# Up projections of both MLPs as seven block products in place of eight

## The chip, the cores and the metric

The kernel runs on one NeuronCore of a Trainium2 chip. The metric is the device time of one execution in microseconds (us). Before the change three executions took 3145.03, 3157.53 and 3156.45 us, a median of 3156.45.

## The reference

One step of a two-layer decoder trunk on 1032 tokens (a prompt of 1024 and eight single new tokens), with D = 1024 and a hidden width of 4096. Layer 0 mixes tokens with a gated DeltaNet and a retention group, layer 1 with a Mamba-2 mixer; behind each mixer stand an output projection and the MLP that the change touches. All is float32.

```python
def squared_relu_mlp(h, w1, w2):
    a = jax.nn.relu(jnp.einsum('bld,df->blf', h, w1))
    return jnp.einsum('blf,fd->bld', a * a, w2)

for layer in range(DEPTH):          # DEPTH = 2
    ...
    x = x + out                     # out: the mixer's projection
    x = x + squared_relu_mlp(rms_norm(x, norm_mlp[layer]), mlp_w1[layer], mlp_w2[layer])
```

## The kernel before, in words

Activations lie transposed: 8 tiles of 128 features by 1032 tokens. Each float32 operand of a large product is held as two parts of the type fp32r, a rounded one (`hi`) and what is left (`lo`). `mm3` (L147) makes one product of 128 features out of three matmuls, hi·hi, hi·lo and lo·hi, with the weights as the stationary operand. `xh` and `xl` hold the parts of the normed activations for the whole kernel (16 tiles).

`load_w` (L135) brings 128x512 weights on SP's DMA queue into one of three `raw` buffers; ScalarE (ACT) rounds them into `whi`, and VectorE (DVE) or GpSimd (POOL) subtracts to get `wlo`. There are buffers for three such pairs (tag `hl`). Products land in PSUM: three banks `pg`, three `pm`, two `ps2`.

`out_proj` (L1335) adds the last blocks of the output projection to eight sum tiles `acc`, which stay in SBUF for the MLP, and splits each finished piece into `xh` and `xl`.

`mlp` (L1216) holds two loops in one. `up(t)` makes one of 32 tiles of 128 hidden features: 8 blocks of features by 3 token slices of 344 columns by 3 matmuls, 72 matmuls. Its eviction clips at zero and multiplies with the norm's factor `rstd_bc` on DVE, squares on ACT (`ahi`) and again on POOL, and subtracts on DVE (`alo`). The parts of hidden tiles stay in SBUF, 14 buffers of 1032 columns. Behind `up(4)`, `up(8)` and so on stands `down(b)`, which adds the products of four hidden tiles to `acc`: 8 output tiles by 3 slices by 4 blocks by 3 matmuls, 288 in all. So no hidden tile leaves the chip. Layer 1 ends with `finish`, which folds the final norm into the last block.

The code is written in one order, and a scheduler sets each engine's order from it; buffers come free when their last reader is done. Each engine then works strictly in its order.

Of the kernel before, what the change touches and what calls it, by code (L numbers as in the profile page):

```python
# [10 lines left out]
F32 = mybir.dt.float32  # L11
F32R = mybir.dt.float32r
# [6 lines left out]
P = 128  # L19
# [47 lines left out]
BLOCK_STEPS = [32, 64]  # L67
HF = 15
SHF = 8
RATE = (0.5, 0.6, 1.5, 0.5, 0.6)  # L70
DG = 2
DS = 2
# [23 lines left out]
class Kern:  # L96
# [330 lines left out]
    def layer(self, l):  # L427
        tc = self.tc
        nk = 16 if l else 8
        with ExitStack() as es:  # L430
            if l == 0:
                self.resid = lambda m: self.I["xT"][:, m, :]
            else:
                self.resid = lambda m: self.resd[m]
            dp = es.enter_context(tc.tile_pool(name=f"spill{l}", bufs=1, space=bass.MemoryType.DRAM))
            self.spill = [dp.tile([P, SEQ], F32, name=f"spill{l}_{k}") for k in range(nk)]
            self.egd = dp.tile([32, SEQ], F32, name=f"egd{l}")
            self.accd = [dp.tile([P, T], F32, name=f"accd{l}_{m}") for m in range(KT)]
            op = es.enter_context(tc.tile_pool(name=f"dec{l}", bufs=1))
            self.dmix = op.tile([P, nk, NDEC], F32, name=f"dmix{l}")  # L440
            name, blocks = ("wos" if l else "woh"), OUT_BLOCKS[l]
            with ExitStack() as es_op:
                with tc.tile_pool(name=f"mixb{l}", bufs=1, side="right", reuse_waits="tile") as gb:
                    with tc.tile_pool(name=f"mixa{l}", bufs=1, reuse_waits="tile") as ga:
                        mixers = (self.ssm_mixers if l else self.hyb_mixers)(Pools(ga, gb))
                        next(mixers)
                    tp = es_op.enter_context(tc.tile_pool(name=f"op{l}", bufs=1, reuse_waits="tile"))
                    next(mixers)
                    parts = self.load_block(blocks[1], tp)
                    for _ in mixers:  # L450
                        pass
                ap = es.enter_context(tc.tile_pool(name=f"acc{l}", bufs=1, side="right", reuse_waits="tile"))
                acc = [ap.tile([P, T], F32, name=f"acc{l}_{m}") for m in range(KT)]
                self.out_proj(name, blocks, acc, tp, parts, "mlp%d" % l)
            self.mlp(l, acc, l == 1)

    def load_block(self, block, tp, pool=None):
        parts = []
# [754 lines left out]
        yield  # L1213


    def mlp(self, l, acc, last):  # L1216
        nc, tc, I = self.nc, self.tc, self.I
        with tc.tile_pool(name=f"mlp{l}", bufs=1, reuse_waits="tile") as tp:
            ssq = self.rstd_bc
            parts = {}  # L1220

            def up(t):
                hi = tp.tile([P, T], F32R, tag="a2", name="ahi", bufs=14)
                lo = tp.tile([P, T], F32R, tag="a2", name="alo", bufs=14)
                parts[t] = (hi, lo)

                def ev(n, ps):
                    s = NSL[n]
                    r = tp.tile([P, NW], F32, tag="r", name="r", bufs=4)
                    nc.vector.scalar_tensor_tensor(out=r, in0=ps, scalar=0.0, in1=self.rstd_bc[:, s], op0=ALU.max, op1=ALU.mult)  # L1230
                    nc.scalar.activation(hi[:, s], r, AF.Square)  # L1231
                    nc.gpsimd.tensor_tensor(out=r, in0=r, in1=r, op=ALU.mult)  # L1232
                    nc.vector.tensor_tensor(out=lo[:, s], in0=r, in1=hi[:, s].bitcast(F32), op=ALU.subtract)  # L1233
                self.gemm_tile(I["w1"][l, t], 128, ev, t == 1)

            def down(b):
                ks = range(4 * b, 4 * b + 4)

                def ev(m, n, ps):
                    s = acc[m][:, NSL[n]]  # L1240
                    nc.vector.tensor_tensor(out=s, in0=s, in1=ps, op=ALU.add)  # L1241
                    if b == HID // 4 - 1:
                        self.split_piece(m, n, s, ssq, tp, "mix1")
                        if n == 2:
                            nc.gpsimd.dma_start(self.resd[m], acc[m])
                for _ in self.gemm_flush(lambda m: I["w2"][l, b, m], [parts.pop(k) for k in ks], ev):
                    pass
            def finish(b):

# [2 lines left out]
                for m in range(KT):  # L1252
                    dst = None
                    if m < 5:
                        w = tp.tile([P, T], F32R, tag="a2", name="wfin", bufs=14)
                        dst = (w[:, 0:512], w[:, 512:1024])
                    ws.append(self.load_w(I["w2"][l, b, m], 512, nc.gpsimd, dst))
                def norm(s0, s1, sqs):
# [62 lines left out]
                    pend = norm(s0, s1, sqs)  # L1321
                for _ in pend:
                    pass
            for t in range(HID):
                up(t)
                if t % 4 == 0 and t:
                    down(t // 4 - 1)
            if last:
                finish(HID // 4 - 1)
            else:  # L1330
# [4 lines left out]
    def out_proj(self, name, blocks, acc, tp, parts, norm):  # L1335
# [3 lines left out]
        with tc.tile_pool(name="oq" + name, bufs=1, side="right", reuse_waits="tile") as tq:  # L1339
# [3 lines left out]
            for i in range(1, len(blocks)):  # L1343
# [3 lines left out]
                def ev(m, n, ps):  # L1347
                    o = acc[m][:, NSL[n]]
                    nc.vector.tensor_tensor(out=o, in0=o, in1=ps, op=ALU.add)  # L1349
                    if last:  # L1350
                        self.split_piece(m, n, o, ssq, tp, norm)
                for _ in self.gemm_flush(lambda m: self.I[name][m, :, c0 * 128:c0 * 128 + w], cur, ev):
                    pass
            self.rstd = self.rstd_from()
# [587 lines left out]
```

## Time and profile before

| what | value |
| --- | --- |
| device time, median of three | 3156.45 us |
| the profiled execution: its own time | 3153.58 us |
| the profiled execution: its span | 3151.8 us |
| matmuls in the span | 19702 |
| ACT busy | 830.7 us (26%) |
| HBM traffic | 174.78 MB read, 43.24 MB written |
| large weight loads of both MLPs (`raw<-w`) | 256, of 256 KB each, median 2.6 us to landing |

How to read it: the page counts an engine as busy while an instruction is in it. Matmuls overlap in the array, so the time that one takes (325 ns for 344 columns) is not the time until the next starts; for that the start times in the timeline have to be subtracted. PEld is the load of the stationary operand, which runs beside the matmuls. "PEclk" is the share of TensorE's clock that was granted.

### The profile page before, as it was taken

To read this page: it belongs to the slowest core of one execution; us is meant where nothing else is said; L and a number is where in the kernel's file an instruction comes from. 1 tells how busy PE (TensorE), PEld (TensorE's weight loads), DVE (VectorE), ACT (ScalarE), POOL (GpSimd) and SP (SyncE) were. 2 spreads that over 40 slices of the span, in tenths; PEclk is the share of its full clock that TensorE was granted. 3 is DMA by queue.
4 is the path that set the end of the run, shared out by engine and by line. 5 is a ranking of instruction groups with operands and counts; after the bars stand their busy time and mean duration, and the time that the engine had idled before them with its cause. 6 is when DMAs were issued, how large, how long until landed. Compare 5 with 4: busy or idle time off the path is not lost. (4 is left out here: it accounts for less than half of the span.)

```text
span 3151.8 us, 48807 instructions
## 1 busy us (share of the span) xinstructions
PE 3031.0 (96%) x19702; PEld 2908.6 (92%) x19702; DVE 1662.4 (53%) x3127; ACT 830.7 (26%) x1577; POOL 922.8 (29%) x940
## 2 busy tenths in 40 slices
PE   8999999989999999999998999999899999999998
PEld 6888888878999999999997989898899999999997
DVE  7664657554333333334778686868435333333334
ACT  4222222214211111113343434343114111111112
POOL 2121214114222112224135444445224222221124
PEclk9899989989999999999999999999999999999999
DMA  4011103153111111112222222224721111111112
GB/s 129 21 49 55 48 22 105 62 178 107 45 47 48 48 48 47 48 48 74 79 66 77 78 98 78 96 77 141 247 74 46 46 48 47 48 48 48 48 47 71
DMA packets 119186, 223.32 MB, mean 71 GB/s; under 512 B 14064, under 2 KB 43504, under 8 KB 118960
## 3 DMA queue, kind: packets, MB, share of 16 engines
q1 hardware_dynamic: 110512, 190.80, 20.0%
q0 software_dynamic: 8448, 29.40, 2.4%
q8 instruction: 155, 2.54, 0.3%
q14 instruction: 71, 0.58, 0.1%
HBM read 174.78 MB, written 43.24 MB: 69 GB/s over the span
## 5 line engine op out<-in xcount | busy, mean ns | idle before, releaser
L148 PE MATMUL pg<-xh,whi 128*128 128x344 f32 x3072 | 999.0, 325 | 2.3 <-DVE z L1525 2.3
L150 PE MATMUL pg<-xh,wlo 128*128 128x344 f32 x3072 | 995.1, 324 | 0.0
L149 PE MATMUL pg<-xl,whi 128*128 128x344 f32 x3072 | 994.6, 324 | 0.0
L142 ACT CAST whi<-raw 128x512 fp32r<-128x512 f32 (+2 forms) x443 | 270.8, 611 | 1215.2 <-PE pg L149 1137.8
L148 PEld LDWEIGHTS pg<-xh,whi 128*128 128x128 f32 x3072 | 582.6, 190 | 9.1 <-DVE z L1525 3.1
L150 PEld LDWEIGHTS pg<-xh,wlo 128*128 128x128 f32 x3072 | 582.7, 190 | 3.4 <-issue 2.3
L149 PEld LDWEIGHTS pg<-xl,whi 128*128 128x128 f32 x3072 | 581.6, 189 | 3.1 <-issue 2.0
L149 PE MATMUL pg<-alo,whi 128*128 128x344 f32 (+2 forms) x1476 | 472.8, 320 | 0.0
L150 PE MATMUL pg<-ahi,wlo 128*128 128x344 f32 (+2 forms) x1476 | 472.7, 320 | 0.0
L148 PE MATMUL pg<-ahi,whi 128*128 128x344 f32 (+2 forms) x1476 | 472.0, 320 | 0.0
L1241 DVE TENSOR_TENSOR acc<-acc,pg 128x344 f32<-128x344 f32 x360 | 183.1, 512 | 387.9 <-PE pg L150 387.7
L143 POOL TENSOR_TENSOR wlo<-raw,whi 128x512 fp32r<-128x512 f32 (+2 forms) x179 | 224.8, 1257 | 507.7 <-ACT whi L142 505.9
L1232 POOL TENSOR_TENSOR r<-r 128x344 f32<-128x344 f32 x192 | 145.9, 760 | 755.3 <-ACT ahi L1231 707.6
L143 DVE TENSOR_TENSOR wlo<-raw,whi 128x512 fp32r<-128x512 f32 x264 | 192.8, 730 | 194.0 <-ACT whi L142 188.1
L150 PEld LDWEIGHTS pg<-ahi,wlo 128*128 128x128 f32 x1476 | 277.9, 188 | 0.0
L148 PEld LDWEIGHTS pg<-ahi,whi 128*128 128x128 f32 x1476 | 277.8, 188 | 0.0
L149 PEld LDWEIGHTS pg<-alo,whi 128*128 128x128 f32 x1476 | 277.6, 188 | 0.0
L1233 DVE TENSOR_TENSOR alo<-r,ahi 128x344 fp32r<-128x344 f32 x192 | 134.7, 702 | 253.6 <-POOL r L1232 253.6
L1231 ACT ACTIVATE ahi<-r 128x344 fp32r<-128x344 f32 x192 | 94.5, 492 | 340.9 <-DVE r L1230 340.9
L148 PE MATMUL pg<-mhi,whi 128*128 128x344 f32 x408 | 132.1, 324 | 8.9 <-DVE acc L1349 6.0
L1230 DVE SCALAR_TENSOR_TENSOR r<-pg,rstd_bc 128x344 f32<-128x344 f32 x186 | 94.9, 510 | 79.4 <-PE pg L150 78.0
L150 PE MATMUL pg<-mhi,wlo 128*128 128x344 f32 x408 | 131.7, 323 | 0.0
(547 smaller groups left out, 4184.7 us busy)
## 6 DMA issues: line engine op xcount, KB each, us to landing
raw<-w SPq DMA_DIRECT2D x256, 256.0 KB, 2.6
raw<-wis SPq DMA_DIRECT2D x80, 256.0 KB, 2.8
raw<-wih SPq DMA_DIRECT2D x56, 256.0 KB, 2.8
mraw<-spill SPq DMA_DIRECT2D x17, 512.0 KB, 4.6
accd<-ost SPq DMA_DIRECT2D x48, 172.0 KB, 3.1
acc<-accd SPq DMA_DIRECT2D x16, 516.0 KB, 7.0
EG<-egd SPq DMA_DIRECT2D x32, 256.0 KB, 6.3
dS<-sstate SPq DMA_DIRECT2D x32, 256.0 KB, 7.1
```

The source lines that it names most:

```text
L142: nc.scalar.copy(hi[:, :n], raw[:, :n])
L143: (lo_eng or nc.vector).tensor_tensor(out=lo[:, :n], in0=raw[:, :n], in1=hi[:, :n].bitcast(F32), op=ALU.subtract)
L148: t.matmul(ps, lhsT=whi, rhs=xhi, start=start, stop=False)
L149: t.matmul(ps, lhsT=whi, rhs=xlo, start=False, stop=False)
L150: t.matmul(ps, lhsT=wlo, rhs=xhi, start=False, stop=stop)
L1230: nc.vector.scalar_tensor_tensor(out=r, in0=ps, scalar=0.0, in1=self.rstd_bc[:, s], op0=ALU.max, op1=ALU.mult)
L1231: nc.scalar.activation(hi[:, s], r, AF.Square)
L1232: nc.gpsimd.tensor_tensor(out=r, in0=r, in1=r, op=ALU.mult)
L1233: nc.vector.tensor_tensor(out=lo[:, s], in0=r, in1=hi[:, s].bitcast(F32), op=ALU.subtract)
L1241: nc.vector.tensor_tensor(out=s, in0=s, in1=ps, op=ALU.add)
```

## The change

Hidden tiles t and t+16 are now made together, as a pair. The weights of the pair are a 2x2 arrangement of blocks (hidden tile t or t+16, features 0-511 or 512-1023), and so are the activations (features 0-511 or 512-1023, token quarters of 258 columns). In place of the eight block products there are seven, of sums and differences of blocks (Strassen's scheme in the form with nested sums), each over 4 feature blocks and 258 columns for each of two token groups. One pair so takes 7 x 4 x 3 x 2 = 168 matmuls of 258 columns, where two `up` took 144 of 344.

- Pairs 1 to 15 are done this way. Tiles 0 and 16 stay plain products and come first; the first pair's weight sums and the sums of the activations are written behind them.
- Activation sums: `out_proj` now stores its eight finished `acc` tiles to DRAM (`accd`). Behind the plain tiles they are loaded again (`ux`), scaled with the norm's weights on ACT, and four sums `ut` for each of four feature blocks are made, two on DVE and two on POOL. Each is split into parts, 32 tiles `t10h` to `t43l` (first digit: the sum, second: the feature block).
- Weight sums: four for each pair on POOL (`sb`, `total`), then seven splits, all with the subtraction on DVE. Nine weight pairs have buffers: three of `hl` and six new ones (`w`).
- Evictions: for each token group of a pair, two copies on ACT and five additions on DVE out of PSUM, two additions on POOL, then clipping and scaling on DVE and squaring on ACT of two pieces of 516 columns. The squared pieces go to DRAM (`hid`), issued on POOL.
- Up and down are apart: `mlp_down` starts when the last pair is done. `acc` is loaded once more into new tiles `res`. Hidden tiles come from `hid` through two buffers `hraw` and are split on ACT and DVE (16 buffers of parts). Hidden tiles 0 and 1 are loaded during pair 5 into the quarters of `xh` and `xl` that no product reads, and `begin` multiplies them first, in pieces of 258 columns: 192 matmuls for what were 144.

```diff
+            self.hid = [dp.tile([P, T], F32, name=f"hid{l}_{k}") for k in range(HID)]
...
-            self.mlp(l, acc, l == 1)
+            self.mlp_up(l)
+            ap = es.enter_context(tc.tile_pool(name=f"res{l}", bufs=1, side="right", reuse_waits="tile"))
+            acc = [ap.tile([P, T], F32, name=f"res{l}_{m}") for m in range(KT)]
+            for m in range(KT):
+                nc.sync.dma_start(acc[m], self.accd[m])
+            self.mlp_down(l, acc, l == 1)
...
+            def out(t, cols, r, n):
+                v.scalar_tensor_tensor(out=r, in0=r, scalar=0.0, in1=self.rstd_bc[:, cols], op0=ALU.max, op1=ALU.mult)
+                a.activation(r, r, AF.Square)
+                nc.gpsimd.dma_start(self.hid[t][:, cols], r)
...
+            plain(0, False)
+            plain(HT, True)
...
+            def parts(x):
+                pool, tag, bufs = (self.wp, "hl", 6) if count < 3 or count % 3 == 0 else (wr, "w", 12)
...
+                a.copy(hi, x)
+                v.tensor_tensor(out=lo, in0=x, in1=hi.bitcast(F32), op=ALU.subtract)
...
+                W = {}
+                a11, a21, a22 = load(t, 0), load(t + HT, 0), load(t + HT, 1)
+                W[1] = parts(a11)
+                s1 = total(a21, a22, ALU.add)
+                s2 = total(s1, a11, ALU.subtract)
+                W[6] = parts(s2)
+                W[5] = parts(s1)
+                s3 = total(a11, a21, ALU.subtract)
+                a12 = load(t, 1)
+                s4 = total(a12, s2, ALU.subtract)
+                yield
+                W[7] = parts(s3)
+                W[4] = parts(a22)
+                W[2] = parts(a12)
+                W[3] = parts(s4)
...
+                for k in range(4):
+                    x = []
+                    for m in (k, k + 4):
+                        r = xp.tile([P, T], F32, tag="x", name="ux", bufs=4)
+                        nc.sync.dma_start(r, self.accd[m])
+                        a.activation(r, r, AF.Copy, scale=self.V(norm, m))
+                        x.append(quarters(r))
...
+                    for j, x0, x1, e in ((1, b12, b11, v), (2, b22, t[1], g), (3, b22, b12, v), (4, t[2], b21, g)):
+                        e.tensor_tensor(out=t[j], in0=x0, in1=x1, op=ALU.subtract)
+                    for j in (2, 1, 3, 4):
+                        hi, lo = TB[j][k]
+                        a.copy(hi, t[j])
+                        v.tensor_tensor(out=lo, in0=t[j], in1=hi.bitcast(F32), op=ALU.subtract)
...
+                c1 = add(a, None, prod(1), None)
+                u2 = add(v, None, prod(6), c1)
+                c5 = add(a, None, prod(5), None)
+                u3 = add(v, None, prod(7), u2)
+                u4 = add(g, None, c5, u2)
+                add(g, r1[:, R], c5, u3)
+                p4 = prod(4)
+                add(v, r1[:, L], u3, p4, ALU.subtract)
+                out(t + HT, cols, r1, 516)
+                add(v, r0[:, L], prod(2), c1)
+                add(v, r0[:, R], prod(3), u4)
+                out(t, cols, r0, 516)
...
+            for t in range(1, HT):
+                pair(t, W, 0)
+                nxt = list(weights(t + 1))[1] if t + 1 < HT else None
+                pair(t, W, 1)
+                W = nxt
...
-            for t in range(HID):
-                up(t)
-                if t % 4 == 0 and t:
-                    down(t // 4 - 1)
+            for k in (2, 3):
+                fetch(k)
+            begin()
+            for b in range(HID // 4 - 1):
+                for k in range(4 * b + 4, 4 * b + 8):
+                    fetch(k)
+                down(b, 0 if b else 2)
...
+                        if n == 2:
+                            nc.sync.dma_start(self.accd[m], acc[m])
```

The scheduler's order is seen at three places, all of layer 0. First, ACT while TensorE is in the first hidden tile; `pm` holds the norm's factors. Before:

```order
L142 CAST whi<-raw 128x512
L272 COPY rstd_bc<-pm 128x512
L275 COPY rstd_bc<-pm 128x8
L272 COPY rstd_bc<-pm 128x512
L1231 ACTIVATE ahi<-r 128x344 x2
L142 CAST whi<-raw 128x512
L1231 ACTIVATE ahi<-r 128x344
```

The same place now (lines are those of the changed file):

```order
L143 CAST whi<-raw 128x512
L1306 ACTIVATE ux<-ux,vec 128x1032 x2
L273 COPY rstd_bc<-pm 128x512
L276 COPY rstd_bc<-pm 128x8
L1314 CAST t10h<-ut 128x516
L1314 CAST t20h<-ut 128x516
L273 COPY rstd_bc<-pm 128x512
L1250 ACTIVATE r<-r 128x344
L1314 CAST t30h<-ut 128x516
L1267 CAST whi<-raw 128x512
L1250 ACTIVATE r<-r 128x344 x2
L1314 CAST t40h<-ut 128x516
```

The scaling of `ux` and the splits of the sums have moved between the plain tiles' own work, behind the split of the second tile's second half of weights (the first row). Second, TensorE behind the two first hidden tiles. Before, the third tile's matmuls stand here, all on parts that lie ready:

```order
L148 MATMUL pg<-xh_71,whi 128x344
L149 MATMUL pg<-xl_79,whi 128x344
L150 MATMUL pg<-xh_71,wlo 128x344
L148 MATMUL pg<-xh_72,whi 128x344
L149 MATMUL pg<-xl_80,whi 128x344
L150 MATMUL pg<-xh_72,wlo 128x344
```

Now it is the first pair, from the point where the last feature block's sums are needed (`ps` is product 5, the first `pm` product 6, the last row product 4):

```order
L151 MATMUL ps<-t12h,wlo 128x258
L149 MATMUL ps<-t13h,whi 128x258
L149 MATMUL pm<-t23h,whi 128x258
L150 MATMUL ps<-t13l,whi 128x258
L151 MATMUL ps<-t13h,wlo 128x258
L150 MATMUL pm<-t23l,whi 128x258
L151 MATMUL pm<-t23h,wlo 128x258
L149 MATMUL pm<-t40h,whi 128x258
```

Here products 5 and 6 of feature blocks 0 to 2 have been done first (30 matmuls of the pair, with product 1), and the matmuls on block 3 stand in the order in which its sums are split. Third, SP's DMA queue at the end of the up projection; before, SP issued nothing but weight loads here, one row for the whole MLP:

```order
L138 DMA raw<-woh 128x384
L138 DMA raw<-woh 128x256
L138 DMA raw<-w 128x512 x128
L1371 DMA raw<-wdt 128x128 x2
L138 DMA raw<-wis 128x512 x5
```

Now:

```order
L139 DMA raw<-w 128x256 x6
L462 DMA res_0_12060<-accd_0_140 128x1032
L462 DMA res_1_12061<-accd_1_141 128x1032
L462 DMA res_2_12062<-accd_2_142 128x1032
L462 DMA res_3_12063<-accd_3_143 128x1032
L462 DMA res_4_12064<-accd_4_144 128x1032
L462 DMA res_5_12065<-accd_5_145 128x1032
L462 DMA res_6_12066<-accd_6_146 128x1032
L462 DMA res_7_12067<-accd_7_147 128x1032
L1386 DMA hraw<-hid_2_109 128x1032
L1386 DMA hraw<-hid_3_110 128x1032
```

The eight loads of `res` stand behind six weight loads of `begin`, of which the sixth has to wait for one of the three `raw` buffers.

More of the change, by code (lines that the diff above doesn't have):

```diff
@@ L69 @@
 SHF = 8
+A2 = 16
 RATE = (0.5, 0.6, 1.5, 0.5, 0.6)
@@ L451, in layer @@
                         pass
-                ap = es.enter_context(tc.tile_pool(name=f"acc{l}", bufs=1, side="right", reuse_waits="tile"))
+                ap = es_op.enter_context(tc.tile_pool(name=f"acc{l}", bufs=1, side="right", reuse_waits="tile"))
                 acc = [ap.tile([P, T], F32, name=f"acc{l}_{m}") for m in range(KT)]
                 self.out_proj(name, blocks, acc, tp, parts, "mlp%d" % l)
-            self.mlp(l, acc, l == 1)
+            self.mlp_up(l)
+            ap = es.enter_context(tc.tile_pool(name=f"res{l}", bufs=1, side="right", reuse_waits="tile"))
+            acc = [ap.tile([P, T], F32, name=f"res{l}_{m}") for m in range(KT)]
+            for m in range(KT):
+                nc = self.nc
+                nc.sync.dma_start(acc[m], self.accd[m])
+            self.mlp_down(l, acc, l == 1)
     def load_block(self, block, tp, pool=None):
@@ L1217, in mlp, with mlp_down @@
+    def mlp_down(self, l, acc, last):
         nc, tc, I = self.nc, self.tc, self.I
@@ L1220, in mlp, with fetch, begin, down @@
             parts = {}
[L1222 to L1237, printed above, removed]
+            def fetch(k):
+                raw = tp.tile([P, T], F32, tag="hraw", name="hraw", bufs=2)
+                nc.sync.dma_start(raw, self.hid[k])
+                hi = tp.tile([P, T], F32R, tag="a2", name="ahi", bufs=A2)
+                lo = tp.tile([P, T], F32R, tag="a2", name="alo", bufs=A2)
+                nc.scalar.copy(hi, raw)
+                nc.vector.tensor_tensor(out=lo, in0=raw, in1=hi.bitcast(F32), op=ALU.subtract)
+                parts[k] = (hi, lo)
+            def begin():
+                for m in range(8):
+                    hi, lo = self.load_w(I["w2"][l, 0, m][:, 0:256], 256, nc.gpsimd)
+                    for j in range(4):
+                        n = slice(258 * j, 258 * j + 258)
+                        ps = self.pg()[:, :258]
+                        for k in range(2):
+                            c = slice(258 + 516 * (j % 2), 516 + 516 * (j % 2))
+                            s = slice(k * 128, k * 128 + 128)
+                            i = 2 * k + j // 2
+                            self.mm3(ps, hi[:, s], lo[:, s], self.xh[i][:, c], self.xl[i][:, c], k == 0, k == 1)
+                        nc.vector.tensor_tensor(out=acc[m][:, n], in0=acc[m][:, n], in1=ps, op=ALU.add)
+            def down(b, k0=0):
+                ks = range(4 * b + k0, 4 * b + 4)
                 def ev(m, n, ps):
@@ L1245, in ev @@
                             nc.gpsimd.dma_start(self.resd[m], acc[m])
-                for _ in self.gemm_flush(lambda m: I["w2"][l, b, m], [parts.pop(k) for k in ks], ev):
+                for _ in self.gemm_flush(lambda m: I["w2"][l, b, m][:, k0 * 128:], [parts.pop(k) for k in ks], ev):
                     pass
@@ L1254, in finish @@
                     if m < 5:
-                        w = tp.tile([P, T], F32R, tag="a2", name="wfin", bufs=14)
+                        w = tp.tile([P, T], F32R, tag="a2", name="wfin", bufs=A2)
                         dst = (w[:, 0:512], w[:, 512:1024])
```

77 lines of the change are left out of this document (76 added, 1 removed).

## The prediction

> **What bounds the kernel now.** I read the page's busy shares first, then its 40 slices, then stage windows over both MLPs, last start times of single matmuls.
>
> ```profile
> span 3151.8 us, 48807 instructions
> PE 3031.0 (96%) x19702; PEld 2908.6 (92%) x19702; DVE 1662.4 (53%) x3127; ACT 830.7 (26%) x1577; POOL 922.8 (29%) x940
> PE   8999999989999999999998999999899999999998
> 775.00:1470.00 695.00, 694.71 (x4420) 694.00 (x4419) 244.94 (x446) 128.31 (x230) 154.41 (x160) 1.00 0.16 47
> 2403.00:3090.00 687.00, 686.99 (x4367) 686.08 (x4366) 240.65 (x434) 123.68 (x221) 151.86 (x158) 1.00 0.16 47
> ```
>
> The last two rows are the windows (length, then busy time and count of PE, PEld, DVE, ACT, POOL, then granted clock). TensorE has no hole in either MLP, at a full clock, while DVE is busy 35% of the time, ACT 18%, POOL 22%. So here time is the number of matmuls times their pitch, and the three other engines have room that the change will use. The pitch comes from start times (a start, a duration, the operation, its columns):
>
> ```profile
> 1000.13 0.32 PE L148 MATMUL pg<-xh,whi 128*128 128x344 f32 x1
> ...
> 1009.56 0.32 PE L148 MATMUL pg<-xh,whi 128*128 128x344 f32 x1
> ...
> 3132.05 0.28 PE L148 MATMUL pg<-ahi,whi 128*128 128x256 f32 x1
> ...
> 3136.19 0.28 PE L150 MATMUL pg<-ahi,wlo 128*128 128x256 f32 x1
> ```
>
> There are 60 steps between the first two, 9.43 / 60 = 157.2 ns for 344 columns; 35 between the last two, 4.14 / 35 = 118.3 ns for 256 columns, each with its own load of 128x128 weights. That is 0.442 ns a column and 5 ns besides; 258 columns then cost 119.2 ns.
>
> **Term 1, the products.** A pair took 144 x 157.2 ns = 22.64 us and takes 168 x 119.2 ns = 20.03 us: 2.61 us less. Fifteen pairs in two layers: **-78.3 us**. `begin` goes the other way, 192 x 119.2 = 22.89 against 144 x 157.2 = 22.64 us: **+0.5 us** for both. The downward products keep their shape.
>
> **Term 2, the wait in the first pair.** The times of both old `up` tiles, from layer 0 (T0 is the first row):
>
> ```profile
> 773.95 0.32 PE L148 MATMUL pg<-xh,whi 128*128 128x344 f32 x1
> 782.15 0.62 ACT L142 CAST whi<-raw 128x512 fp32r<-128x512 f32 x1 [5.88 <-PE pg L149]
> 802.62 0.49 ACT L1231 ACTIVATE ahi<-r 128x344 fp32r<-128x344 f32 x1 [1.09 <-DVE r L1230]
> ```
>
> The two plain tiles end at about T0+28.1 (the last square starts 0.51 us of DVE later). ACT's order has `ux` behind the cast that starts at T0+8.2, so the activation sums start at T0+8.8, and what they need in all must fit into some 19 us. What it costs:
>
> ```profile
> L1534 ACT ACTIVATE z<-x 128x1032 f32<-128x1032 f32 x16 | 17.0, 1065 | 49.6 <-POOL x L1533 49.6
> L423 ACT ACTIVATE th<-z 128x516 f32<-128x516 f32 x48 | 30.4, 634 | 84.4 <-DVE z L1525 54.4 <-DVE z L496 22.0 <-DVE z L424 4.0
> L142 ACT CAST whi<-raw 128x512 fp32r<-128x512 f32 x419 | 259.4, 619 | 1159.2 <-PE pg L149 1097.8 <-PE ps L149 14.0 <-issue 13.6
> L424 DVE SCALAR_TENSOR_TENSOR z<-th,z 128x516 f32<-128x516 f32 x48 | 34.0, 709 | 14.3 <-ACT th L423 14.3
> L143 DVE TENSOR_TENSOR wlo<-raw,whi 128x512 fp32r<-128x512 f32 x264 | 192.8, 730 | 194.0 <-ACT whi L142 188.1
> L143 POOL TENSOR_TENSOR wlo<-raw,whi 128x512 fp32r<-128x512 f32 x155 | 203.0, 1310 | 429.4 <-ACT whi L142 427.6 <-DMA mraw<-spill 1.7
> L293 DVE TENSOR_TENSOR dg<-rh,c 128x256 fp32r<-128x256 f32 x35 | 14.8, 422 | 5.3 <-PE pm L295 3.7 <-PE ps L295 0.4
> 824.22 1.29 POOL L143 TENSOR_TENSOR wlo<-raw,whi 128x512 fp32r<-128x512 f32 x1
> 824.26 1.63 DVE L1233 TENSOR_TENSOR alo<-r,ahi 128x344 fp32r<-128x344 f32 x1 [1.46 <-POOL r L1232]
> ```
>
> The last two rows matter most. A DVE subtraction of two SBUF operands starts 0.04 us after a POOL operation and ends 0.38 us behind its end, though its median alone is 0.518. The two engines did not work side by side; one queued behind the other. So I add their times up. Until the split of sum 2 of the last feature block, the `t23l` that product 6 needs, DVE has 8 sums, 14 splits and 3 weight splits, each about 0.38 x 516 / 344 = 0.57 us when queued, and 6 of the norm's `dg` at 0.42: 14.3 + 2.5 = 16.8 us. POOL has 8 activation sums and 4 weight sums, 12 x 1.31 = 15.7 us. Together 32.5 us from T0+9.5 (cast and its subtraction done): T0+42. With 1 us for waits between engines, T0+43. TensorE has 30 matmuls of the pair until then, 3.6 us, and stands from T0+31.7: 11.3 us. Product 4 needs two more splits and that of its weights: +1.5 us. Product 3's split stands behind the second pair's on ACT and DVE, and those wait for loads into `raw` buffers that products 4 and 2 have just released: the loads (2.6 us) and three sums (3.9 us) end some 2.5 us after TensorE gets there.
>
> A wait this long has an after-effect:
>
> ```profile
> 2244.25 0.39 PE L148 MATMUL pg<-ohi,whi 128*128 128x344 f32 x1 [2.83 <-DVE ost L482]
> 2245.45 0.49 PE L148 MATMUL pg<-ohi,whi 128*128 128x344 f32 x1
> ...
> 2248.03 0.49 PE L148 MATMUL pg<-ohi,whi 128*128 128x344 f32 x1
> 2245.03:2248.44 3.41, 3.41 (x14) 3.41 (x13) 0.51 (x1) 0.00 (x0) 0.66 (x1) 0.50 1.02 391
> ```
>
> After 2.83 us without work the granted clock is 0.50 for 3.41 us and 9 steps take 2.58 us, 287 ns each: 12 matmuls cost 1.6 us more. Sum for a layer: 11.3 + 1.5 + 2.5 + 1.6 = 17 us, **+34 us** for both. Bounds: ACT alone (8 x 1.065 + 14 x 0.634 + 3 x 0.62 + 6 x 0.49 + 1.3 for the norm = 23.5 us, T0+32.3) would leave 4 us a layer; with every DVE operation at its full 0.73 behind POOL, 24 us.
>
> **Term 3, from up to down.** `begin` needs `res`, and the loads stand on SP behind a weight load that waits for a `raw` buffer, which is free when POOL has split `begin`'s third weights. Those need the buffer that product 4 of the last pair reads, until 2.85 us before the pair's end (two products). With cast and split (1.2 us) the loads go out 1.5 us before the end.
>
> ```profile
> 2265.52 4.15 DMA acc<-accd
> acc<-accd SPq DMA_DIRECT2D x16, 516.0 KB, 7.0
> ```
>
> The first of eight such loads took 4.15 us where it was waited for (the chain), so `res` is there 2.7 to 3 us behind the last product. TensorE fills three banks in 3 x 6 x 0.119 = 2.1 us and then waits for an addition of 0.4 us: 1.3 us, taken as 1.5. **+3 us** for both; bounds 0 and, with all eight loads to land first (7 us), 5 each. `hid` loads follow on SP, but are first needed 23 us later.
>
> **Small ones.** Four loads of `hid` in pair 5 use the three `r` buffers that the evictions use: +0.5 a layer. `finish` used to have three `up` tiles between the last full `down` and itself, in which its weights were split; now the first split by POOL (1.31 us) comes when `down` ends: +1. **+2 us.** The eight stores of `accd` stand on SP ahead of weight loads, but those weights are used three tiles later (17 us at 36 matmuls a tile): 0.
>
> **What is hidden in the pairs.** In 20.03 us DVE has 7 splits, 4 scalings of 516 columns and 10 additions out of PSUM, ACT 7 casts, 4 copies and 4 squares, POOL 4 sums of 512, 4 additions of 258 and 4 DMA issues:
>
> ```profile
> L1309 DVE TENSOR_TENSOR acc<-acc,pg 128x256 f32<-128x256 f32 x8 | 3.2, 415 | 1.9 <-PE pg L150 1.9
> L1279 ACT COPY rsl<-pm 128x256 f32<-128x256 f32 x1 | 0.4, 372 | 3.9 <-PE pm L295 3.9
> L1283 POOL TENSOR_TENSOR acc<-acc,rsl 128x256 f32<-128x256 f32 x3 | 2.1, 727 | 2.2 <-ACT rsl L1279 2.2
> L1784 POOL DMA_DIRECT2D o_sssm<-dS x32 | 18.5, 579 | 22.6 <-DVE dS L1783 22.6
> ```
>
> DVE: 7 x 0.73 + 4 x 0.71 + 10 x 0.415 = 12.1 us. ACT: 7 x 0.62 + 4 x 0.37 + 4 x 0.63 = 8.3. POOL: 4 x 1.31 + 4 x 0.73 + 4 x 0.58 = 10.5. None reaches 20. DVE's operations on two SBUF operands (7.95) and POOL's sums (8.16) exclude each other: 16.1 of 20. A late eviction costs nothing at first, since seven products use eight banks and a bank is needed again 5 us or more after its product. I take 0 and keep 1 us a pair as the far bound.
>
> **Sum.** -78.3 + 0.5 + 34 + 3 + 2 = -38.8 us. The profiled execution took 3153.58 us, so it would take 3114.8; the median shown is 2.9 us above it, so I forecast 3117 us, own range 3103 to 3132.
>
> **Rivals.** *The first pair is covered* (chance 0.22): engines queue less than added up, and ACT's list sets the end. Then some 7.5 us a layer: -78.3 + 0.5 + 15 + 5 = -58, 3098 us. For it: the scheduler put this work between the plain tiles' own; many DVE rows show no delay. Against: the pair of rows at 824.
>
> *The pairs lose a little each* (0.13): 0.3 to 1.3 us a pair in DVE's strict order, +9 to +39 us: 3126 to 3156.
>
> *The port sets the pace* (0.07), slower than before: if DVE's 12.1 us and POOL's 8.2 us never overlap, and POOL's issues (2.3 us) exclude DVE too, a pair needs 22.6 us, 2.5 more than its products; 30 pairs cost 76, in all +37: 3194 us. It decides from 38.8 / 30 = 1.3 us over, 21.3 us a pair. Against it: additions out of PSUM ran beside POOL. [...]
>
> *A matmul costs by number, not by columns* (0.03): at an unchanged 157.2 ns a pair takes 26.4 us, 3.8 more: 113 + 39 = +152, 3309 us; it turns the result from 127 ns on. The rows at 3132 say 118. The Trainium skill ("TensorE: Matmul & The Clock Gate", section "Back-to-back issue gap") gives sustained streams as 81 ns at 128 columns and 131 at 512; an estimate between them is 109 at 344 and 98 at 258, by which a pair would get slower, 15.7 to 16.4 us, and the change with it. Both pitches measured here are longer and nearly proportional to the columns, so they decide.
>
> **How the numbers follow.** Forecast 0.50, the rivals 0.22, 0.13, 0.07, 0.03, something else 0.05. The range 3092 to 3150 reaches from the covered case with 4 us a layer to most of the third case and leaves out 0.2. About 0.5%, 16 us, can be told from no change: faster than 3140.7 are the forecast, the covered case, half of the third and a little of the rest, 0.80; within 0.10; slower 0.10.
>
> **What would show it.** In the pairs, 258-column matmuls 119 ns apart without holes (term 1); in each first pair, TensorE waiting 15 us for DVE's `t23l` and then DVE's `wlo`, with POOL and DVE taking turns (term 2); 1 to 2 us before the first additions into `res` (term 3). A TensorE share under 95% in the middle of the up stage, or holes at every pair, would prove the sum wrong; so would a clock below 1.00 there.

## The result, and the profile after

| | before | after |
| --- | --- | --- |
| device time, median of six runs | 3155.25 us | 3134.84 us |
| lowest to highest | 3145.03 to 3165.01 | 3129.65 to 3140.15 |
| the profiled execution: its own time, its span | 3153.58, 3151.8 | 3136.73, 3134.8 |

The ratio is 0.9931, with a 95% interval from 0.9914 to 0.9948: faster by 0.7%, or 20 us. The forecast was 3117 us with a range of 3092 to 3150, so the sign and the range held, and the gain was half of what was forecast.

The page of the changed kernel, its span, busy shares, TensorE's slices and the granted clock in slices:

```profile
span 3134.8 us, 52481 instructions
PE 2983.4 (95%) x20518; PEld 2854.7 (91%) x20518; DVE 1893.3 (60%) x3445; ACT 990.2 (32%) x1859; POOL 1162.9 (37%) x1152
PE   8999999988899999999998999999899999999998
PEclk9889989889999999999999999999999999999999
```

There are 816 matmuls more, but TensorE's busy time has fallen by 48 us and its share from 96 to 95%. Two stage windows of the changed kernel (length, busy time and count of PE, PEld, DVE, ACT, POOL, clock, DMA share, GB/s), one in the pairs and one over the first pair of layer 0, show how much the two stages differ:

```profile
840.00:880.00 40.00, 40.00 (x336) 40.00 (x335) 23.93 (x43) 14.53 (x29) 22.65 (x26) 1.00 0.33 114
805.00:830.00 25.00, 18.09 (x94) 16.09 (x94) 19.26 (x26) 12.03 (x21) 12.08 (x11) 0.73 0.21 64
```

In the pairs TensorE has no hole at a full clock; the median distance of two starts there is 120 ns. In the first pair it works 72% of the time at a mean clock of 0.73.

To find where the rest went, I subtracted from the distance of each two starts the pitch that the prediction took for the first one's columns (157.2 ns at 344, 119.2 at 258, and so on). What is left is what a stage lost. In us, layer 0 / layer 1:

| kernel | plain tiles | first pair | other pairs | `begin` | first block of down |
| --- | --- | --- | --- | --- | --- |
| after, first profile | 2.8 / 6.9 | 14.4 / 12.4 | 3.8 / 4.3 | 5.1 / 3.5 | 1.7 / 5.2 |
| after, second profile | 2.0 / 7.2 | 15.3 / 10.9 | 1.7 / 1.7 | 5.0 / 5.1 | 1.4 / 4.0 |

Before, the first two tiles lost 1.2 / 0.7 us, the rest of up and down 0.8 / 0.6 and `finish` with the end 5.7. The changed kernel's later blocks of down lose 1.3 in both layers together and `finish` with the end 4.9. So the first profile lost 66.3 us where 9.0 were lost before, 57.3 more. The products themselves are 77.8 us shorter (-78.3, and +0.5 in `begin`). That leaves -20.5 in the two MLPs; 3.5 us more outside them (1.8 between the MLPs, 1.7 at the end) make the -17.0 between the two spans.

The rows of the first pair of layer 0 in the changed kernel's timeline, TensorE's first, then DVE's and POOL's:

```profile
808.62 0.58 PE L150 MATMUL pm<-t22l,whi 128*128 128x258 f32 x1 [3.22 <-DVE t22l L1315]
812.23 0.58 PE L149 MATMUL ps<-t13h,whi 128*128 128x258 f32 x1 [0.71 <-ACT t13h L1314]
814.15 0.58 PE L149 MATMUL pm<-t23h,whi 128*128 128x258 f32 x1 [1.33 <-ACT t23h L1314]
815.65 0.58 PE L150 MATMUL pm<-t23l,whi 128*128 128x258 f32 x1 [0.48 <-DVE t23l L1315]
...
812.31 1.68 DVE L1315 TENSOR_TENSOR t13l<-ut,t13h 128x516 fp32r<-128x516 f32 x1
814.13 1.47 DVE L1315 TENSOR_TENSOR t23l<-ut,t23h 128x516 fp32r<-128x516 f32 x1
815.52 0.68 DVE L1315 TENSOR_TENSOR t33l<-ut,t33h 128x516 fp32r<-128x516 f32 x1
...
811.81 1.63 POOL L1311 TENSOR_TENSOR ut<-ux,ut 128x516 f32<-128x516 f32 x1 [1.40 <-ACT ux L1306]
813.52 1.52 POOL L1311 TENSOR_TENSOR ut<-ut,ux 128x516 f32<-128x516 f32 x1
```

TensorE waits for the sums' splits in the order of the feature blocks. The two DVE subtractions that run while POOL sums take 1.68 and 1.47 us, and end 0.55 and 0.56 us behind the end of the POOL sum that was running when they started; the third, with POOL done, takes 0.68. So each seems to have waited for POOL's sum and then to have run. `t23l` is ready at 815.6, 41.7 us after the first matmul of the layer's MLP.

A stage that the prediction had priced at nothing is the first plain tile of layer 1. The norm's `dg` goes through DVE there (DVE's rows, one of POOL's, and one of TensorE's):

```profile
2401.40 1.09 DVE L294 TENSOR_TENSOR dg<-rh,c 128x256 fp32r<-128x256 f32 x1 [0.24 <-PE pm L296]
2402.41 1.42 DVE L294 TENSOR_TENSOR dg<-rl,c 128x256 fp32r<-128x256 f32 x1
2403.75 1.77 DVE L1311 TENSOR_TENSOR ut<-ux 128x516 f32<-128x516 f32 x1
2405.45 1.48 DVE L294 TENSOR_TENSOR dg<-rh,c 128x256 fp32r<-128x256 f32 x1
2406.86 1.48 DVE L294 TENSOR_TENSOR dg<-rl,c 128x256 fp32r<-128x256 f32 x1
...
2405.05 1.60 POOL L1280 TENSOR_TENSOR sb<-sb,raw 128x512 f32<-128x512 f32 x1
...
2406.99 0.58 PE L296 MATMUL pm<-dg,ones_r 128*128 128x256 f32 x1 [1.78 <-DVE dg L294]
```

An activation sum stands between the norm's operations, POOL makes weight sums beside them, and a `dg` takes up to 1.48 us where 0.42 was its mean before. TensorE waited up to 1.78 us for one of them.

The other place is `begin`. ACT's rows there in layer 0, TensorE's, and one of DVE's:

```profile
1137.47 1.06 ACT L1389 CAST ahi<-hraw 128x1032 fp32r<-128x1032 f32 x1 [6.66 <-DMA hraw<-hid]
1138.83 1.05 ACT L1389 CAST ahi<-hraw 128x1032 fp32r<-128x1032 f32 x1 [0.30 <-DMA hraw<-hid]
1139.79 1.02 ACT L143 CAST whi<-raw 128x256 fp32r<-128x256 f32 x3
...
1140.28 0.36 PE L149 MATMUL pg<-xh,whi 128*128 128x258 f32 x1 [1.22 <-ACT whi L143]
1141.91 0.39 PE L151 MATMUL pg<-xh,wlo 128*128 128x258 f32 x1 [1.16 <-POOL wlo L144]
...
1160.10 1.23 DVE L1390 TENSOR_TENSOR alo<-hraw,ahi 128x1032 fp32r<-128x1032 f32 x1 [1.82 <-ACT ahi L1389]
...
1161.90 0.39 PE L149 MATMUL pg<-ahi,whi 128*128 128x344 f32 x1 [1.32 <-DVE res L1412]
```

The casts of two hidden tiles wait 6.66 us for a load, and three weight casts of `begin` stand behind them on ACT. At 1160 the same happens on DVE: an addition out of PSUM, for which TensorE waits 1.32 us, stands behind the subtraction of a hidden tile.

### The profile page after: what moved, and what is told of

The parts are those of the page before. It is cut to its first block, busy times and chain, and to the rows that moved or that the text cites. A ratio compares the mean times of both kernels' runs of the same rounds, so it can differ in the third digit from the quotient of the medians.

```text
span 3134.8 us, 52481 instructions
## 1 busy us (share of the span) xinstructions
PE 2983.4 (95%) x20518; PEld 2854.7 (91%) x20518; DVE 1893.3 (60%) x3445; ACT 990.2 (32%) x1859; POOL 1162.9 (37%) x1152
## 5 line engine op out<-in xcount | busy, mean ns | idle before, releaser
L149 PE MATMUL pg<-xh,whi 128*128 128x344 f32 (+1 forms) x2240 | 714.2, 319 | 9.6 <-ACT c L1341 2.4
L151 PE MATMUL pg<-xh,wlo 128*128 128x344 f32 (+1 forms) x2240 | 709.1, 317 | 3.6 <-POOL wlo L144 2.3
L150 PE MATMUL pg<-xl,whi 128*128 128x344 f32 (+1 forms) x2240 | 708.8, 316 | 0.0
L149 PE MATMUL pg<-ahi,whi 128*128 128x344 f32 (+1 forms) x1380 | 441.9, 320 | 4.4 <-DVE res L1412 4.4
L149 PEld LDWEIGHTS pg<-xh,whi 128*128 128x128 f32 x2240 | 428.2, 191 | 18.8 <-ACT c L1341 3.9
L151 PE MATMUL pg<-ahi,wlo 128*128 128x344 f32 (+1 forms) x1380 | 442.4, 321 | 0.0
L150 PE MATMUL pg<-alo,whi 128*128 128x344 f32 (+1 forms) x1380 | 441.3, 320 | 0.0
L151 PEld LDWEIGHTS pg<-xh,wlo 128*128 128x128 f32 x2240 | 428.3, 191 | 8.1 <-POOL wlo L144 2.7
L150 PEld LDWEIGHTS pg<-xl,whi 128*128 128x128 f32 x2240 | 428.4, 191 | 3.5 <-issue 2.2
L1412 DVE TENSOR_TENSOR res<-res,pg 128x344 f32<-128x344 f32 x360 | 182.6, 511 | 323.7 <-PE pg L151 322.7
```

What stands on the lines that cost most here:

```text
L149: t.matmul(ps, lhsT=whi, rhs=xhi, start=start, stop=False)
L150: t.matmul(ps, lhsT=whi, rhs=xlo, start=False, stop=False)
L151: t.matmul(ps, lhsT=wlo, rhs=xhi, start=False, stop=stop)
```

## The experiments

All are edits of the changed kernel. Times are medians; ratios are to the kernel before, measured beside them. The executions of one kernel lie 6 to 19 us apart and the interval of a ratio is 5 to 7 us to each side, so a difference of less than some 8 us between two edited kernels is not shown by the times alone. There the losses of the stages, each from one profiled execution, have to decide.

### The other pairs: chance or order

The kernel again, without an edit.

> The changed kernel once more, unchanged, for a second profile. In its first profile pairs 3 to 15 lost 3.7 and 4.2 us over a pitch of 119.2 ns, in holes of up to 1.2 us where a weight sum on POOL waited for a weight load; four kernels with the same pairs lost 1.6. If a load's landing time makes these holes by chance, they are gone or elsewhere here (1.6 to 3 us a layer) and the time is 3130 to 3140; if the changed order around the pairs makes them, they stand at the same pairs with the same 4 us.

It took 3133.73 us, ratio 0.9932 (0.9914 to 0.9951). The holes at pairs 3 to 15 were gone, and what is left, 1.7 us a layer, is a pitch of 119.9 ns in place of 119.2. In the first profile such a hole looked like this:

```profile
1005.80 1.28 POOL L1280 TENSOR_TENSOR sb<-raw 128x512 f32<-128x512 f32 x1 [1.50 <-DMA raw<-w]
...
1009.95 0.39 PE L149 MATMUL pg<-xh,whi 128*128 128x258 f32 x1 [0.93 <-ACT c L1341]
```

A weight load landed late, the sum on POOL with it, then a cast on ACT, and behind that cast in ACT's order the copy that frees a bank. It comes and goes between executions of one program, so it is chance. In the nine other kernels below these pairs lost 1.6 to 3.0 us a layer. Beyond the pitch the pairs have no loss of their own.

### Do DVE and POOL exclude each other

All activation sums on DVE, and in a second kernel all on POOL:

```diff
-((1, b12, b11, v), (2, b22, t[1], g), (3, b22, b12, v), (4, t[2], b21, g))
+((1, b12, b11, v), (2, b22, t[1], v), (3, b22, b12, v), (4, t[2], b21, v))
...
+((1, b12, b11, g), (2, b22, t[1], g), (3, b22, b12, g), (4, t[2], b21, g))
```

> The changed kernel with all sixteen activation sums of a layer on DVE, none on POOL. Theory (the two engines exclude each other on operands in SBUF): eight sums of 1.2 to 1.6 us on POOL go and eight of 0.68 us on DVE come, and DVE's splits beside them fall from 1.5 to 0.68 us; the split t23l comes 3 to 6 us earlier, and the first pair's 14.2 and 12.3 us become 8 to 11: 3 to 10 us under 3134.8. Rival (the engines work side by side, DVE's own list sets the end): DVE has 5.4 us more to do before t23l, the first pair waits 5 us longer in each layer: 3145.

> The changed kernel with all sixteen activation sums of a layer on POOL, none on DVE: the other side of sums_on_dve. Theory (the two engines exclude each other on operands in SBUF): eight sums of 0.6 us leave DVE and eight of 1.3 us come to POOL, so that both together have 5.6 us more; t23l comes 4 to 6 us later and plain tiles and first pair lose that much more in each layer (17.2 and 19.3 us over the pitch in the first profile, 17.3 and 18.1 in the second): 8 to 12 us above 3134, about 3144. Rival (side by side, DVE's own list sets the end): DVE has 4.8 us less to do, and 5 to 10 us go: about 3127.

| activation sums on POOL, a layer | 0 | 8 (after, first / second) | 16 |
| --- | --- | --- | --- |
| `t23l` ends behind the MLP's first matmul, layer 0 | 38.6 us | 41.7 / 41.9 | 45.4 |
| the same, layer 1 | 38.3 | 42.8 / 42.8 | 45.0 |
| plain tiles and first pair lost, both layers | 30.5 | 36.5 / 35.4 | 44.4 |
| median | 3127.14 us | 3134.84 / 3133.73 | 3141.69 |
| ratio | 0.9925 (0.9905 to 0.9945) | 0.9931, 0.9932 | 0.9951 (0.9933 to 0.9969) |

Each eight sums taken off DVE and given to POOL made the end later, by 3.4 us on average (38.5, 42.3, 45.2 as the means of both layers). If the engines worked side by side and DVE's list set the end, it would have been the reverse. The intervals of the three ratios overlap; it is the end of `t23l` that separates the kernels, and it differs by 0.2 us or less between the two profiles of the changed kernel. With sixteen sums POOL is itself busy for 28.49 of the 32 us from 795 to 827, so its own longer list may have a part in that end. The exclusion is seen in single rows. A split from each kernel's timeline shows it; first with the sums on DVE, with POOL idle, then with the sums on POOL:

```profile
816.17 0.69 DVE L1315 TENSOR_TENSOR t23l<-ut,t23h 128x516 fp32r<-128x516 f32 x1
```

```profile
812.23 1.69 DVE L1315 TENSOR_TENSOR t21l<-ut,t21h 128x516 fp32r<-128x516 f32 x1
...
811.71 1.66 POOL L1311 TENSOR_TENSOR ut<-ut,ux 128x516 f32<-128x516 f32 x1
813.33 1.56 POOL L1311 TENSOR_TENSOR ut<-ux 128x516 f32<-128x516 f32 x1
```

With the sums on DVE that engine is the bound by itself, and ACT has time left. The window over the first pair of that kernel, and behind it that of the changed kernel:

```profile
800.00:820.00 20.00, 15.22 (x84) 13.26 (x83) 19.86 (x33) 15.37 (x26) 3.45 (x5) 0.83 0.39 142
```

```profile
796.00:816.00 20.00, 13.97 (x77) 12.58 (x77) 19.36 (x23) 14.45 (x23) 10.90 (x10) 0.81 0.45 155
```

DVE, the third pair of numbers, is full in both, with 33 operations in the one and 23 in the other. The exclusion is shown, and with it that the sums' end is set by DVE and POOL together, not by ACT's list, whose work is the same in all three kernels. The first pair was expected to fall to 8 to 11 us a layer, and did not: it lost 12.9 in layer 0 and 14.4 in layer 1, together no less than before the edit. All of the 6 us are in the plain tiles (9.7 to 3.2 us in both layers), where `dg` no longer queues behind POOL's activation sums. In layer 1 the plain tiles end 5.7 us earlier and `t23l` only 4.5, so the first pair has longer to wait.

### The norm first

The sums' work on DVE and ACT is queued behind the norm's last `dg` and last copy:

```diff
-            with tc.tile_pool(name=f"upx{l}", bufs=1, side="right", reuse_waits="tile") as xp:
+            with tc.tile_pool(name=f"upx{l}", bufs=1, side="right", reuse_waits="tile") as xp, \
+                    tc.issue_after(self.last_dg.ins), tc.issue_after(self.last_rc.ins):
```

> The changed kernel with the activation sums' work on DVE and ACT queued behind the norm's last dg and its last copy to rstd_bc. Theory (order): the holes in the first plain tile (2.8 us over the pitch in layer 0, 6.9 in layer 1, against 1.2 and 0.7 before) come from sums and splits that stand between the norm's dg on DVE and are themselves slowed by POOL; they go, and the first pair pays back less than half, since ACT and DVE had idle time: 3 to 7 us under 3134.8. Rival (fixed work): what starts later ends later by as much, and the first pair waits 2 to 6 us longer in each layer: within 2 us of 3134.8.

3128.86 us, ratio 0.9923 (0.9907 to 0.9938). The view of the tile `dg` in layer 1 of this kernel (min, median and max ns of one operation) shows that the holes' cause is gone:

```profile
L294 DVE TENSOR_TENSOR dg<-rh,c x4: 419/425/427, 2392.2 to 2397.4; 128x256 fp32r<-128x256 f32 x4
L294 DVE TENSOR_TENSOR dg<-rl,c x4: 418/418/428, 2392.5 to 2397.9; 128x256 fp32r<-128x256 f32 x4
```

The plain tiles lose 1.2 / 0.7 us, as before the change. But the first pair loses 17.0 / 17.1: plain tiles and first pair together are 36.0 us, against 36.5 and 35.4 in the two profiles of the changed kernel. The median, 6 us lower, is within the expectation of the first theory, but the ratios differ by only 2.5 us and their intervals overlap, so the time does not tell the kernels apart. The stages speak for the rival: what starts later ends later.

### More cover

```diff
             plain(0, False)
             plain(HT, True)
+            plain(1, False)
+            plain(HT + 1, True)
```

Weight sums and pairs begin with tile 2, so there are fourteen pairs.

> The changed kernel with four plain tiles (0, 16, 1, 17) ahead of fourteen pairs, in place of two and fifteen. Theory (cover): the first pair waits because some 32 us of sums and splits on DVE and POOL do not fit beside 22.6 us of plain products; with 45 us of them the wait of 14.2 and 12.3 us over the pitch goes down to 0 to 2 us a layer, at a price of 2.6 us a layer for the products saved less: 18 to 21 us under 3134.8, about 3115. Rival (order): the scheduler spreads the same work over the longer time, or a load sets the end; then the wait stays, and the kernel is 5 us slower, 3140.

3117.86 us, ratio 0.989 (0.987 to 0.9911), 17 us under the changed kernel. The first pair loses 3.8 / 4.3 us and the plain tiles 2.5 / 1.8, 24 us less than before this edit; the price was 5.2. The first pair was expected at 0 to 2 us a layer. What stays are short waits for weight splits, such as

```profile
829.43 0.39 PE L151 MATMUL ps<-t10h,wlo 128*128 128x258 f32 x1 [0.76 <-DVE wlo L1270]
```

So the wait was for the most part a lack of cover, not an order that fills whatever time it is given.

### Hidden tiles' loads out of the way

```diff
-            for k in (2, 3):
-                fetch(k)
             begin()
...
+                    if m in (3, 5):
+                        fetch(2 + (m > 3))
...
+                with tc.issue_after(self.last_cast.ins), tc.issue_after(self.last_add.ins):
                     nc.scalar.copy(hi, raw)
                     nc.vector.tensor_tensor(out=lo, in0=raw, in1=hi.bitcast(F32), op=ALU.subtract)
```

`last_cast` and `last_add` are the newest weight cast and the newest addition into `res`. `down` calls `fetch` in the same way after every second output tile.

> The changed kernel with one thing moved: the loads of hidden tiles in the down projection are written between the output tiles (two in begin, four in each down), and their casts and subtractions are queued on ACT and DVE behind the weight cast and the addition of the output tile just done, so that they no longer stand ahead of them. Theory (order): the holes between the last pair and the second block of down, 6.8 us over the pitch in layer 0 and 7.8 in layer 1, come from casts on ACT and subtractions on DVE that wait for a hidden tile's load while begin's weight casts and the additions into res stand behind them; then 10 to 13 us go against the changed kernel's 3134.8 (about 3123). Rival (bandwidth): 5.3 MB of res and hidden tiles take some 18 us wherever their casts stand, so TensorE stands as long at another place: within 3 us of 3134.8.

3126.47 us, ratio 0.9916 (0.9896 to 0.9936), 8.4 us less by the medians and less than the 10 to 13 expected. `begin` and the first block of down lose 6.9 us in both layers together, where the two profiles of the changed kernel lost 15.5 each and the profiles of `sums_on_dve`, `sums_on_pool` and `norm_first`, with the same order here, 12.7 to 14.4. So 6 to 9 us were a matter of order. Not all of it went, since in `begin` the casts still came ahead of the last three weight casts.

What is left shows TensorE in `begin`, in layer 0 and 1 of this kernel, waiting for the first addition into `res`:

```profile
1121.94 0.38 PE L149 MATMUL pg<-xh,whi 128*128 128x258 f32 x1 [0.84 <-DVE res L1406]
2741.30 0.39 PE L149 MATMUL pg<-xh,whi 128*128 128x258 f32 x1 [2.25 <-DVE res L1406]
```

So `begin`'s products were given eight banks in place of three, on top of this edit:

```diff
-                        ps = self.pg()[:, :258]
+                bk = [self.pg, self.pm, self.ps2]
...
+                        ps = bk[(4 * m + j) % 3]()[:, :258]
```

> The kernel with the hidden tiles' loads spread (hid_spread), and begin's products in all eight PSUM banks in turn, where they were in three. Theory (res is late): TensorE fills three banks and then waits for the first addition into res, 1.1 us in layer 0 and 2.5 in layer 1; five more banks are 3.6 us of work, so both holes go: 2 to 4 us under hid_spread's 3126.5. Rival (bandwidth of the eight res loads): the holes come at a later output tile; within 1 us of 3126.5.

3127.98 us, ratio 0.9908 (0.9888 to 0.9929): no gain that can be measured against the kernel it was built on. `begin` loses 3.8 / 3.7 us where it lost 2.6 / 2.9. The holes at the first addition went, and one at a weight cast behind the hidden tiles grew, in layer 0 to

```profile
1135.43 0.38 PE L149 MATMUL pg<-xh,whi 128*128 128x258 f32 x1 [1.46 <-ACT whi L143]
```

The time is 1.5 us over `hid_spread`'s, and the holes came later, as the rival has it; whether bandwidth or order makes the later hole is asked again below.

### All together

Four plain tiles, sums on DVE and behind the norm, hidden loads spread, eight banks; and the same with two of the four sums on POOL.

> All together: four plain tiles, hidden loads spread, begin in eight banks, the activation sums on DVE and behind the norm. If the causes are separate, the holes over the pitch of four_plain (39 us in both layers) fall by about 10 in begin, 3 in the first block of down and 5 to 8 in the plain tiles and the first pair: 18 to 21 us under four_plain's 3117.9, about 3099. If they share one limit (DVE's list or the loads), less than half of it: over 3108.

> As combined, but two of the four activation sums stay on POOL. Theory (DVE and POOL exclude each other): with 45 us of plain products the sums still end later, and the first pair stands 2 to 4 us longer in each layer than in combined: 4 to 8 us above it. Rival (four plain tiles cover the work either way): within 2 us of combined.

`combined` took 3109.84 us, ratio 0.9859 (0.984 to 0.9878); `combined_pool` 3117.27, ratio 0.9881 (0.9861 to 0.9901), 7.4 us more by the medians. Of that the first pair has 4.7 (7.3 / 5.3 against 3.3 / 4.6); in the two profiles another 4.8 lie ahead of the first MLP, where the kernels are the same. The exclusion costs here too, but not in the way that was expected: the first pair does not wait for the sums. `t23l` ends 39.5 us behind the MLP's first matmul in layer 0 (38.9 in `combined`), 10 us before the first pair begins. TensorE waits for a weight cast, which stands on ACT behind a cast whose load came late (TensorE, ACT and DVE of `combined_pool` in layer 0):

```profile
831.81 0.39 PE L149 MATMUL pm<-t20h,whi 128*128 128x258 f32 x1 [2.80 <-ACT whi L1269]
...
830.62 0.62 ACT L1269 CAST whi<-raw 128x512 fp32r<-128x512 f32 x1 [4.76 <-DMA raw<-w]
...
809.39 1.82 DVE L144 TENSOR_TENSOR wlo<-raw,whi 128x512 fp32r<-128x512 f32 x1
```

A weight load needs a free `raw` buffer, and DVE's split of the weights before it frees one. Beside POOL's sums two of these splits took 1.69 and 1.82 us, where they took 0.69 and 0.68 in `combined`, and the third of the first pair's weight loads went out 40.2 us behind the MLP's first matmul in place of 35.1. In layer 1 the first pair lost only 0.7 us more than in `combined`, less than the 2 to 4 expected.

`combined` is 8.0 us under `four_plain`, and so in the second case, with less than half of 18 to 21: plain tiles 1.1 / 0.9 and down 0.7 / 0.7 came out, but `begin` lost 7.4 / 6.8. ACT in layer 1 of this kernel, and two of its windows:

```profile
2731.12 1.05 ACT L1393 CAST ahi<-hraw 128x1032 fp32r<-128x1032 f32 x1 [8.20 <-DMA hraw<-hid]
2732.49 1.05 ACT L1393 CAST ahi<-hraw 128x1032 fp32r<-128x1032 f32 x1 [0.31 <-DMA hraw<-hid]
2733.45 1.02 ACT L143 CAST whi<-raw 128x256 fp32r<-128x256 f32 x3
```

```profile
2720.00:2725.00 5.00, 5.00 (x44) 5.00 (x43) 2.91 (x9) 0.41 (x1) 1.07 (x2) 1.00 1.01 410
2725.00:2730.00 5.00, 5.00 (x44) 5.00 (x43) 3.60 (x10) 0.00 (x0) 0.00 (x0) 1.00 1.03 419
```

The DMA engines are full (the share behind the clock) at 410 to 419 GB/s with the loads of `res` and of hidden tiles, and a cast waits 8.20 us for its load, with three weight casts behind it. So the last edit orders these too:

```diff
+                    nc.sync.dma_start(acc[m], self.accd[m])
                     hi, lo = self.load_w(I["w2"][l, 0, m][:, 0:256], 256, nc.gpsimd)
...
-                    if m in (3, 5):
-                        fetch(2 + (m > 3))
+                    if m > 5:
+                        fetch(m - 4)
```

> As combined, but the loads of res are written one to an output tile of begin, and the first two hidden tiles' loads and casts behind its seventh and eighth output tile, where they were behind the fourth and sixth. In combined begin lost 7.4 and 6.8 us over the pitch, since ACT's cast of a hidden tile waited 8.2 us for its load with three weight casts of begin behind it, while the DMA engines were full. Theory (order): the weight casts now stand ahead of it, begin loses 1 to 3 us, and 8 to 12 us go against combined's 3109.8, about 3100. Rival (bandwidth): begin's last weights are loaded behind 4.2 MB of res anyway, and begin loses 5 us or more: 3106 to 3111.

3103.86 us, ratio 0.9828 (0.9812 to 0.9843): `begin` loses 0.5 / 0.9 us, so the order was its cause, with the same 4.2 MB of `res` to load; 2.5 us came back in the first block of down (2.6 / 1.3). The edit moves the loads of `res` and the hidden tiles at once, and which of the two did it stays open. By the medians 6.0 us went, less than the 8 to 12 expected; by the ratios, 10. This kernel is 1.7% below the kernel before and, by the medians, 31 us below the changed one.

## Why the prediction was right in sign and forecast twice the gain

| term of the sum, both layers | forecast | first profile | second profile |
| --- | --- | --- | --- |
| products, `begin` | -77.8 | -77.8, and +3.4 for a pitch of 119.9 | the same |
| plain tiles | 0 | +7.8 | +7.3 |
| first pair | +34 | +26.8 | +26.2 |
| holes in the other pairs | 0 | +4.7 | 0 |
| up to down | +3 | +15.5 | +15.5 |
| `finish`, four `hid` loads | +2 | -0.8 | not taken |
| outside the MLPs | 0 | +3.5 | not taken |

**Term 1 held.** The pitch was forecast at 119.2 ns and is 119.9, 3.4 us over the other pairs of both layers. A matmul did cost by its columns here.

**Term 2 held in its mechanism and roughly in its size.** The prediction gave T0+43 for `t23l`, and it came at T0+41.7; it had TensorE standing from T0+31.7, and it stands from 805.4, T0+31.5, first for block 2's splits and then for block 3's. Layer 0's 14.4 us are 9.2 until `t23l` (11.3 forecast), none for product 4 (1.5), 2.1 for product 3 (2.5), and 3.1 of half clock in between (1.6). In all 38 matmuls ran at half clock in layer 0 and 29 in layer 1, for 3.7 and 2.8 us; why so many is in the last section.

**What the sum left out** is that the same added work stands in the *first* plain tile too, between the norm's `dg`. The prediction read the row that shows a DVE operation queued behind POOL and applied it to the splits that follow, but not to the `dg` that share those queues, though its count of DVE's work lists six of them. The cost is 7 to 8 us. It is real, but not free to take back: `norm_first` moved it into the first pair, which then lost 34.1 us. Plain tiles and first pair together lost 34.6 us more than before in the first profile, and 34 were forecast: the cost of the sums was right in total, and part of it was paid at another place.

**Term 3 is the one that failed**, with 3 us forecast and 15.5 found. Its own step, `res` landing behind the last product, is right: 0.84 and 2.25 us of waiting in `begin` once the rest is gone, 1.5 forecast. The wrong step is "`hid` loads follow on SP, but are first needed 23 us later". A load that is needed late brings a cast and a subtraction that stand early in the strict orders of ACT and DVE, and those were not read. 6 to 9 us went with their place alone, and in `combined_2` nearly all of `begin`'s loss.

**The pairs' steady state** was rightly put at 0: no engine reaches 20 us, and the 1.3 us a pair at which the change would have turned slower is far off. Pairs 5 and 6, beside the four `hid` loads, lost 0.11 to 0.13 us each, which is their pitch, where 0.5 was forecast. The rival by which the port sets the pace is refuted for the pairs. The exclusion on which it rests is real and sets the end of the sums, but its other condition is not: in the changed kernel's trace 75 of the pairs' DVE operations on two SBUF operands ran beside a DMA issue of POOL and no sum, and none took over 0.70 us. The rival of the covered first pair, with 7.5 us a layer, rested on ACT's list as the limit; the two kernels with the sums moved refute that. It was nearly covered only with four plain tiles.

**The chances.** The forecast's own range, 3103 to 3132, was missed by 3 us, and the outer one held. Between the -38.8 of the sum and the -17.0 of the two profiles lie 12.5 us of term 3, 4.7 of holes that came by chance, 3.4 of pitch and 3.5 outside the MLPs, whose cause stays open; `finish` gave 2.8 back. That the sums came out at 34.6 against 34 is in part luck: in layer 0 the half clock cost 3.7 us where 1.6 was forecast, and product 4 nothing where 1.5 was. Luck too is that the time lies in the band of the rival in which the pairs lose a little each: it got there by other causes.

**Two bounds do not come out of their own terms.** With 25 DVE operations at 0.73 us the first pair would cost 21 us a layer, not 24. And the covered first pair stands at 4 us a layer in the bound, but at 7.5 in the rival. The forecast uses neither.

## What to carry to other kernels

A saving in the steady state is earned only where a stage is steady: here 78 us of products saved came with 50 us at three seams: the plain tiles (7.8), the first pair (26.8) and the step from up to down (15.5). For each added load, follow not only when its data is needed but where the cast behind it stands in its engine's order, and who stands behind that. And when a split of work between DVE and POOL looks balanced, look whether both take both operands from SBUF; here, where they did, giving all of it to the engine with the shorter instruction ended `t23l` some 4 us earlier.

## What the runs showed of the hardware

**DVE and POOL.** With two SBUF operands of 516 columns DVE takes 0.68 to 0.69 us alone and 1.47 to 1.77 beside POOL in the rows above, and POOL's own sums take 1.52 to 1.66 there. An addition with one operand in PSUM is not delayed: 87 of the pairs' DVE additions of 258 columns ran beside a POOL sum in the changed kernel's trace, and none took over 0.43 us. I had expected turns, but not where the wait shows: it is counted in DVE's own duration, so a DVE that looks full, at 19.36 of 20 us, waited in some 5.5 of them. That is an estimate: its 23 operations, at the 0.60 us that the 33 took on average, are 13.8.

**The clock after short waits.** Three windows of the changed kernel behind the first wait of layer 0:

```profile
808.60:815.65 7.05, 4.50 (x16) 3.52 (x16) 6.63 (x9) 5.28 (x9) 3.70 (x3) 0.50 0.08 27
815.65:822.03 6.38, 6.38 (x29) 6.26 (x29) 3.30 (x6) 2.15 (x6) 0.45 (x1) 0.50 0.26 82
822.03:830.00 7.97, 6.83 (x51) 6.13 (x50) 5.73 (x7) 2.90 (x5) 6.23 (x6) 1.00 0.24 68
```

One wait of 2.8 us was followed by 3.41 us at half clock in the kernel before. Here a wait of 3.22 us was followed by three more of 0.5 to 1.3, and the clock stayed at 0.50 for 13.4 us, of which the last 6.4 had no wait. The Trainium skill ("TensorE: Matmul & The Clock Gate", section "Part 1: The HAM clock gate") says that the clock is released after a busy window of about 3.4 us, and that the window runs free of the program; 6.4 us would fit that if a window that has begun with a wait does not count, since nearly two windows may then pass; no run here tests it. At half clock 258 columns took 215 ns, 1.79 times the 119.9 at full clock.

**DMA.** In `combined` one core alone moved 410 to 419 GB/s over 10 us, for the most part loads from DRAM, through 16 engines that were busy all the time. The Trainium skill ("DMA: Bandwidth & Descriptors", section "Specifications") gives 435 GB/s as the ceiling of the fabric and some 358 as one core's limit of HBM; the measured rate is above the second, which so did not bound this core, and near the first.
